# Log-sum-exp over heads: seven batches' results in one store behind the loads, and hand-named waits on the x buffers

## The chip, the cores and the metric

One core of one Trainium2 chip. The metric is the device time of one execution in microseconds (us), the median of 10 runs. All arithmetic is float32 except a bias that is split into bfloat16 parts.

## What is computed

```python
B, S, D, H = 8, 2048, 2048, 8
x_heads = x.reshape(B, S, H, D // H).transpose(0, 2, 1, 3)
x_heads = x_heads + bias[None, :, None, :]
x_tiled = np.repeat(x_heads, 2, axis=2)
mx = x_tiled.max(axis=-1, keepdims=True)
lse = mx.squeeze(-1) + np.log(np.exp(x_tiled - mx).sum(axis=-1))
```

For each of 8 batches, 2048 rows and 8 heads, 256 numbers plus their head's bias go through exp, are summed, and the log of the sum is written twice in a row. The input is 134 MB, the output (8, 8, 4096) float32 is 1 MB. The kernel leaves out the maximum, since exp of these inputs does not overflow.

## The kernel before, in words

**Tiles and loads.** The work is cut into T = 64 tiles of 256 rows by 2048 columns (2 MB), 8 tiles to a batch. Each partition holds K = 2 rows. Nine buffers `xt0` to `xt8` (`NBUF`, line 17) take the tiles in turn. `load(t)` (line 101) issues one DMA for each piece of a tile, always from SyncE's queue (SP). Up to tile 56 a tile is one piece; from tile 57 on it is two halves of 1 MB (one for each row of a partition); the last tile is cut into six pieces of 256 to 512 KB (`LAST_CUTS`, line 29). The load of tile t+9 is issued after the last instruction that uses tile t (line 328).

**Who does what to a tile.** There are three modes (lines 23 to 27). In all of them the first `pe` heads are done by TensorE and ScalarE: `add_bias` (line 158) puts the bias into PSUM with a small bfloat16 matmul, adds x to it with a matmul by the identity (line 177), and `sum_biased` (line 186) takes exp of each head with the sum as a by-product (line 189). The heads from `g0` up get their bias from GpSimd, in place (`g_add`, line 204, recorded at 207), then exp in place on ScalarE (`later`, line 214, exp at 212) and a sum on VectorE (line 228). The heads between are exp'd without bias and weighted by exp(bias):
- BULK, tiles 0 to 48: pe=2, g0=4. Heads 2 and 3 are multiplied by their weight in place on VectorE (line 222) before the sum over heads 2 to 7 (line 228).
- MIXED, tiles 49 to 60: pe=1, g0=5. Heads 1 to 4 are weighted and summed by `weigh` (line 235), one custom VectorE instruction for each row and head (line 240) which writes the weighted values to one of two scratch buffers `junk` and the sum to the results.
- PROMPT, tiles 61 to 63: pe=2, g0=8. GpSimd has no part; heads 2 to 7 go through `weigh`.

**Results.** The sums of batch b are gathered in `R[b]`. Two tiles after a batch's last tile, `finish(b)` (line 251) transposes them on TensorE (line 258), takes the log on ScalarE into one of two buffers `res0`, `res1`, 64 partitions by 2 KB (line 268), and stores 128 KB from SP's queue (line 269). `finish_last` (line 274) does the same for batch 7 into `res_last` with a store of its own (line 283).

**What sets the order.** The order of each engine's instructions is the order in which the program issues them (`manual_schedule`, line 107). A framework adds the waits: it tracks who wrote and who read each buffer, and gives an instruction a semaphore wait for every engine and DMA it depends on. Work of the engine itself can be waited for too: VectorE's `weigh` waits for the earlier `weigh` that wrote the same `junk`. DMAs on SP take 8 semaphores in turn ("lanes"), and a DMA waits for the DMA eight places before it on SP. An instruction holds one wait itself; for more, EVENT_SEMAPHORE instructions stand in front of it. The stores of batches 0 to 5 stand on SP between loads: behind the load of tile 17, 25, 33, 41, 49 and the second half of 57. The store of batch 6 already stands behind all loads.

Of the kernel before, what the change touches and what calls it, by code (L numbers as in the profile page):

```python
# [9 lines left out]
F32 = mybir.dt.float32  # L10
BF16 = mybir.dt.bfloat16
ACT = mybir.ActivationFunctionType
# [3 lines left out]
K = 2  # L16
NBUF = 9
# [15 lines left out]
def kernel(  # L33
# [6 lines left out]
    nc = tc.nc  # L40
    P = nc.NUM_PARTITIONS
    B, S, D = x.shape
    H, Dh = bias.shape
    assert D == H * Dh and S % (P * K) == 0
    NBLK = S // (P * K)
    T = B * NBLK
# [5 lines left out]
    sb = ctx.enter_context(tc.tile_pool(name="sb", bufs=1))  # L52
# [13 lines left out]

    R = [sb.tile([P, K, H, NBLK], F32, name=f"R{b}") for b in range(B - 1)]
    R_last = sb.tile([P, H, NBLK, K], F32, name="R_last")
    junk = [sb.tile([P, Dh], F32, name=f"junk{i}") for i in range(2)]
    res = [sb.tile([H * NBLK, P, K, 2], F32, name=f"res{i}") for i in range(2)]  # L70
    res_last = sb.tile([P, P, 2], F32, name="res_last")
    xts = [sb.tile([P, K, D], F32, name=f"xt{i}") for i in range(NBUF)]
    w_ps = pp.tile([P, W1 - W0], F32, name="w_ps")
# [4 lines left out]
    def mode_of(t):  # L78
        return [m for t0, m, _ in STAGES if t0 <= t][-1]

    def halves_of(t):
        return [s for t0, _, s in STAGES if t0 <= t][-1]

    def pieces(t):

        if not halves_of(t):
            return [(0, K, 0, D)]
        cuts = [[0, D]] * K if t < T - 1 else LAST_CUTS
        return [
            (k, k + 1, c0, c1) for k in range(K) for c0, c1 in zip(cuts[k], cuts[k][1:])  # L90
        ]

    def rows_of(t):

        b, blk = divmod(t, NBLK)
        v = x[b, blk * P * K : (blk + 1) * P * K, :]
        if b < B - 1:
            return v.rearrange("(p k) d -> p k d", k=K)
        return v.rearrange("(k p) d -> p k d", k=K)

    def load(t):
        for k0, k1, c0, c1 in pieces(t):
            nc.sync.dma_start(  # L103
                out=xts[t % NBUF][:, k0:k1, c0:c1], in_=rows_of(t)[:, k0:k1, c0:c1]
            )

    order = tc.manual_schedule()
# [3 lines left out]
    for set_idx, (_name, funcs) in enumerate(get_activation_tables(nc.m.arch).items()):  # L111
        if ACT.Exp in funcs and ACT.Ln in funcs:
            nc.scalar.add_instruction(
                mybir.InstLoadActFuncSet(
                    name=nc.get_next_instruction_name(),
# [5 lines left out]
    for t in range(NBUF):  # L121
        load(t)
# [20 lines left out]
    for i, c in enumerate(range(G0, D, MM)):  # L143
        spread(ps[i], c, c + MM)
        nc.scalar.activation(  # L145
            out=b_rep[:, c - G0 : c - G0 + MM], in_=ps[i], func=ACT.Copy
# [6 lines left out]


    n_ps = [0]
    n_junk = [0]

    def add_bias(m, xt, k0, k1):

        n = m["pe"] * Dh  # L160
        step = MM // n
        groups = [(k, min(k + step, k1)) for k in range(k0, k1, step)]
        got = []
        for ka, kb in groups:
            p = ps[n_ps[0] % len(ps)]
            n_ps[0] += 1
            nc.tensor.matmul(  # L167
                p[:, 0 : (kb - ka) * n],
                lhsT=ones3,
                rhs=each_row(b3, 0, n, kb - ka),  # L170
                start=True,
                stop=False,
            )
            got += [p[:, k * n : (k + 1) * n] for k in range(kb - ka)]
        for ka, kb in groups:
            p = got[ka - k0]
            nc.tensor.matmul(  # L177
                bass.AP(tensor=p.tensor, offset=p.offset, ap=[p.ap[0], [1, (kb - ka) * n]]),
                lhsT=ident,
                rhs=xt[:, ka:kb, 0:n],  # L180
                start=False,
                stop=True,
            )
        return got

    def sum_biased(m, p, dst):
        for h in range(m["pe"]):
            c = h * Dh
            nc.scalar.activation(  # L189
                out=p[:, c : c + Dh],  # L190
                in_=p[:, c : c + Dh],
                func=ACT.Exp,
                accum_out=dst(h),
            )

    def each_row(src, c, n, k_rows):

        return bass.AP(
            tensor=src.tensor,
            offset=src.offset + c,  # L200
            ap=[src.ap[0], [0, k_rows], [1, n]],
        )

    def g_add(m, xt, k0, k1):
        c = m["g0"] * Dh
        v = xt[:, k0:k1, c:D]
        nc.gpsimd.tensor_tensor(  # L207
            out=v, in0=v, in1=each_row(b_rep, c - G0, D - c, k1 - k0), op=ALU.add
        )

    def exp_inplace(v):
        nc.scalar.activation(out=v, in_=v, func=ACT.Exp)  # L212

    def later(m, xt, k0, k1, sums):

        h0 = m["pe"] if m["late"] else m["g0"]
        v = xt[:, k0:k1, h0 * Dh : D]
        exp_inplace(v)
        if m["late"]:
            n = (m["g0"] - h0) * Dh  # L220
            f = v[:, :, 0:n]
            nc.vector.tensor_tensor(  # L222
                out=f,
                in0=f,
                in1=each_row(w_ps, h0 * Dh - W0, n, k1 - k0),
                op=ALU.mult,
            )
        nc.vector.tensor_reduce(  # L228
            out=sums[:, k0:k1, h0:H],
            in_=v.rearrange("p k (h j) -> p k h j", j=Dh),  # L230
            op=ALU.add,
            axis=mybir.AxisListType.X,
        )

    def weigh(v, h, dst):
        c = h * Dh
        w = w_ps[:, c - W0 : c - W0 + Dh] if c < W1 else w_sb[:, c - W1 : c - W1 + Dh]
        j = junk[n_junk[0] % 2]
        n_junk[0] += 1
        nc.vector.tensor_tensor_reduce(  # L240
            out=j,
            in0=v,
            in1=w,
            scale=1.0,
            scalar=0.0,
            op0=ALU.mult,
            op1=ALU.add,
            accum_out=dst,
        )

    def finish(b):

        nr = H * NBLK
        n = P * K * 2
        tp = tps[b % 2]
        rs = res[b % 2]
        for k in range(K):
            nc.tensor.transpose(  # L258
                out=tp[0:nr, k],
                in_=R[b][:, k].rearrange("p h n -> p (h n)"),  # L260
                identity=ident,
            )
        tv = bass.AP(
            tensor=tp.tensor,
            offset=tp.offset,
            ap=[[tp.ap[0][0], nr], [1, P], [P, K], [0, 2]],
        )
        nc.scalar.activation(out=rs[0:nr], in_=tv, func=ACT.Ln)  # L268
        nc.sync.dma_start(
            out=out[b].rearrange("h (n r) -> (h n) r", r=n),  # L270
            in_=rs[0:nr].rearrange("q p k r -> q (p k r)"),
        )

    def finish_last():
# [14 lines left out]
    def sums_of(t):  # L289

        b, blk = divmod(t, NBLK)
        if b < B - 1:
            return R[b][:, :, :, blk]
        return R_last[:, :, blk, :].rearrange("p h k -> p k h")
# [3 lines left out]
    for t in range(T):  # L298
        m = mode_of(t)
        xt = xts[t % NBUF]  # L300
        sums = sums_of(t)
        for k0, k1, c0, c1 in pieces(t):
            if c0 == 0:
                got = add_bias(m, xt, k0, k1)
                if m["g0"] < H:
                    g_add(m, xt, k0, k1)
            if for_pool:
                for_pool()
                for_pool = None
            h0 = max(c0 // Dh, m["pe"])  # L310
            h1 = min(c1 // Dh, m["g0"])
            if h0 < h1 and not m["late"]:
                exp_inplace(xt[:, k0:k1, h0 * Dh : h1 * Dh])
            if for_pe and (c0 == 0 or c1 == D):
                for_pe()
                for_pe = None
            if not m["late"]:
                for k in range(k0, k1):
                    for h in range(h0, h1):
                        weigh(  # L320
                            xt[:, k, h * Dh : (h + 1) * Dh], h, sums[:, k, h : h + 1]
                        )

            def pool_part(t=t, m=m, xt=xt, k0=k0, k1=k1, sums=sums):
                if m["g0"] < H:
                    later(m, xt, k0, k1, sums)
                if k1 == K and t + NBUF < T:
                    load(t + NBUF)

            def pe_part(m=m, got=got, k0=k0, k1=k1, sums=sums):  # L330
                for k in range(k0, k1):
                    sum_biased(m, got[k - k0], lambda h: sums[:, k, h : h + 1])

            for_pool = pool_part
            if c0 == 0:
                if m["g0"] < H:
                    pe_part()
                else:
                    for_pe = pe_part

        fb, at = divmod(t - 2, NBLK)
        if fb >= 0 and at == NBLK - 1:
            finish(fb)
    for_pe and for_pe()
    finish_last()

# [31 lines left out]
```

The softmax here doesn't subtract the row's maximum and nothing guards it: scores larger than these inputs give would overflow.

## Time and profile before

| | |
|---|---|
| median of 10 runs | 332.18 us (331.91 to 332.39) |
| the profiled execution's own time | 332.26 us |
| its span, first to last instruction | 330.5 us |
| DMA queue of SP (q1): share of 16 engines' span | 96.9% |
| HBM read, written | 134.23 MB, 1.05 MB |
| instructions in the trace | 2287 |
| VectorE's EVENT_SEMAPHORE at line 240 | 24 |
| SP's EVENT_SEMAPHORE at line 103 | 107, 17 to 28 ns each |
| GpSimd's EVENT_SEMAPHORE at line 207 | 53, 17 to 43 ns each |
| ScalarE's EVENT_SEMAPHORE at line 212 | 65, 17 ns each |

Engines are PE (TensorE), PEld (its weight loads), DVE (VectorE), ACT (ScalarE), POOL (GpSimd) and SP. A "q" behind an engine's name (SPq) is its instruction queue. In a row of the timeline come start, duration, engine and line, what is written and read, and in brackets the idle time before it on its engine and what ended it. Here 1.8 us of the execution lie outside the span. In the rows of stages (windows) the fields are the stage, its length, each engine's busy time with its number of instructions, TensorE's granted clock, the mean busy share of the 16 DMA engines, and GB/s.

### The profile page before, as it was taken

To read this page: it belongs to the slowest core of one execution; us is meant where nothing else is said; L and a number is where in the kernel's file an instruction comes from. 1 tells how busy PE (TensorE), PEld (TensorE's weight loads), DVE (VectorE), ACT (ScalarE), POOL (GpSimd) and SP (SyncE) were. 2 spreads that over 40 slices of the span, in tenths; PEclk is the share of its full clock that TensorE was granted. 3 is DMA by queue.
4 is the path that set the end of the run, shared out by engine and by line. 5 is a ranking of instruction groups with operands and counts; after the bars stand their busy time and mean duration, and the time that the engine had idled before them with its cause. 6 is when DMAs were issued, how large, how long until landed. Compare 5 with 4: busy or idle time off the path is not lost. (4 is left out here: it accounts for less than half of the span.)

```text
span 330.5 us, 2287 instructions
## 1 busy us (share of the span) xinstructions
PE 230.5 (70%) x383; PEld 66.0 (20%) x383; DVE 288.2 (87%) x380; ACT 291.3 (88%) x567; POOL 270.7 (82%) x79
## 2 busy tenths in 40 slices
PE   5499667676767689666896766967946545665790
PEld 2122211121211122211221221321211110132220
DVE  0019999999999999999999999989889999999994
ACT  2269999999999989989989999998999998999894
POOL 6999989979989999899999999988998667786300
PEclk9999896598777855898558777595697555555577
DMA  7999999999999999999999999999999999999970
GB/s 295 433 424 436 428 425 430 426 426 428 419 437 427 428 428 426 429 429 428 427 428 428 424 432 424 430 430 425 432 424 427 432 424 420 417 421 424 415 277 18
DMA packets 11745, 135.43 MB, mean 410 GB/s; under 512 B 1425, under 2 KB 1553, under 8 KB 2769
## 3 DMA queue, kind: packets, MB, share of 16 engines
q1 hardware_dynamic: 11632, 135.27, 96.9%
q14 instruction: 12, 0.10, 0.1%
q8 instruction: 3, 0.05, 0.1%
q10 hardware_dynamic: 2, 0.01, 0.0%
q0 software_dynamic: 96, 0.00, 0.0%
HBM read 134.23 MB, written 1.05 MB: 409 GB/s over the span
## 5 line engine op out<-in xcount | busy, mean ns | idle before, releaser
L207 POOL TENSOR_TENSOR xt<-xt,b_rep 128x2048 f32<-128x2048 f32 (+2 forms) x65 | 264.3, 4068 | 35.6 <-DMA xt<-in_x_dram 28.8
L177 PE MATMUL ps<-xt,ident 128*128 128x512 f32 (+1 forms) x240 | 175.9, 865 | 71.5 <-DMA xt<-in_x_dram 71.0
L212 ACT ACTIVATE xt<-xt 128x3072 f32<-128x3072 f32 (+3 forms) x89 | 184.6, 2095 | 9.6 <-POOL xt L207 7.7
L228 DVE TENSOR_REDUCE R<-xt 128x12 f32<-128x3072 f32 (+1 forms) x56 | 176.6, 3154 | 5.8 <-DVE xt L222 1.0
L189 ACT ACTIVATE ps<-ps 128x256 f32<-128x256 f32 x232 | 85.7, 369 | 15.9 <-PE ps L177 11.3
L222 DVE TENSOR_TENSOR xt<-xt,w_ps 128x1024 f32<-128x1024 f32 x49 | 59.6, 1217 | 30.0 <-ACT xt L212 29.9
L177 PEld LDWEIGHTS ps<-xt,ident 128*128 128x128 f32 x240 | 54.2, 255 | 153.2 <-DMA xt<-in_x_dram 110.1
L167 PE MATMUL ps<-b,ones 3*128 3x512 bf16 (+1 forms) x120 | 49.1, 473 | 9.0 <-ACT ps L189 5.3
L189 ACT ACTIVATION_READ_ACCUMULATOR ps<-ps 128x1 f32 x232 | 44.2, 190 | 0.0
L240 DVE CUSTOM_DVE_ANT_0 junk<-xt,w_ps 128x256 f32<-128x256 f32 x114 | 40.6, 418 | 1.2 <-ACT xt L212 1.1
L167 PEld LDWEIGHTS <-ones 3*128 3x128 bf16 x120 | 7.9, 98 | 80.2 <-issue 80.2
L228 DVE TENSOR_REDUCE R_last<-xt 128x3 f32<-128x768 f32 (+1 forms) x9 | 9.4, 1042 | 0.0
L258 PE MATMUL tpair<-ident,R 128*64 128x128 f32 x14 | 3.7, 361 | 7.5 <-DVE R L228 6.0
L240 DVE CUSTOM_DVE_ANT_0 junk<-xt,w_sb 128x256 f32<-128x256 f32 x18 | 6.7, 422 | 0.0
L240 DVE DVE_READ_ACCUMULATOR2_ANT R_last<- 128x1 f32 x76 | 6.5, 85 | 0.0
L139 PE MATMUL ps<-brow,ones 1*128 1x512 f32 x4 | 3.7, 1085 | 3.5 <-DMA brow<-in_bias_dram 3.5
L145 ACT ACTIVATE b_rep<-ps 128x512 f32<-128x512 f32 x2 | 1.2, 597 | 4.6 <-PE ps L139 4.6
L240 DVE DVE_READ_ACCUMULATOR2_ANT R<- 128x1 f32 x56 | 4.7, 85 | 0.0
L139 PE MATMUL w_ps<-brow,ones 1*128 1x512 f32 x4 | 4.0, 1094 | 0.7 <-ACT w_ps L151 0.7
L258 PEld LDWEIGHTS tpair<-ident,R 128*64 128x64 f32 x14 | 1.5, 138 | 14.3 <-DVE R L228 11.0
L268 ACT ACTIVATE res<-tpair 64x512 f32<-64x512 f32 x7 | 4.1, 581 | 0.2
L151 ACT ACTIVATE w_ps<-w_ps 128x512 f32<-128x512 f32 x2 | 1.2, 582 | 3.3 <-PE w_ps L139 3.3
(21 smaller groups left out, 12.4 us busy)
## 6 DMA issues: line engine op xcount, KB each, us to landing
xt<-in_x_dram SPq DMA_DIRECT2D x57, 2048.0 KB, 31.7
xt<-in_x_dram SPq DMA_DIRECT2D x12, 1024.0 KB, 20.8
out_dram<-res SPq DMA_DIRECT2D x7, 128.0 KB, 31.0
xt<-in_x_dram SPq DMA_DIRECT2D x3, 256.0 KB, 15.7
xt<-in_x_dram SPq DMA_DIRECT2D x2, 384.0 KB, 15.9
xt<-in_x_dram SPq DMA_DIRECT2D x1, 512.0 KB, 12.3
out_dram<-res_last SPq DMA_DIRECT2D x1, 128.0 KB, 1.7
b<-bparts POOLq DMA_DIRECT2D x3, 1.0 KB, 5.6
```

The costliest lines, as they stand in the source:

```text
L139: nc.tensor.matmul(dst, lhsT=ones, rhs=brow[:, c0:c1], start=True, stop=True)
L145: nc.scalar.activation(out=b_rep[:, c - G0 : c - G0 + MM], in_=ps[i], func=ACT.Copy)
L167: nc.tensor.matmul(p[:, 0 : (kb - ka) * n], lhsT=ones3, rhs=each_row(b3, 0, n, kb - ka), start=True, stop=False,)
L177: nc.tensor.matmul(bass.AP(tensor=p.tensor, offset=p.offset, ap=[p.ap[0], [1, (kb - ka) * n]]), lhsT=ident, rhs=xt[:, ka:kb, 0:n], start=F ...
L189: nc.scalar.activation(out=p[:, c : c + Dh], in_=p[:, c : c + Dh], func=ACT.Exp, accum_out=dst(h),)
L207: nc.gpsimd.tensor_tensor(out=v, in0=v, in1=each_row(b_rep, c - G0, D - c, k1 - k0), op=ALU.add)
L212: nc.scalar.activation(out=v, in_=v, func=ACT.Exp)
L222: nc.vector.tensor_tensor(out=f, in0=f, in1=each_row(w_ps, h0 * Dh - W0, n, k1 - k0), op=ALU.mult,)
L228: nc.vector.tensor_reduce(out=sums[:, k0:k1, h0:H], in_=v.rearrange("p k (h j) -> p k h j", j=Dh), op=ALU.add, axis=mybir.AxisListType.X,)
L240: nc.vector.tensor_tensor_reduce(out=j, in0=v, in1=w, scale=1.0, scalar=0.0, op0=ALU.mult, op1=ALU.add, accum_out=dst,)
L258: nc.tensor.transpose(out=tp[0:nr, k], in_=R[b][:, k].rearrange("p h n -> p (h n)"), identity=ident,)
L268: nc.scalar.activation(out=rs[0:nr], in_=tv, func=ACT.Ln)
```

## The change

Three edits. First, `res` becomes one buffer of 64 partitions by 7 batches by 2 KB, `finish(b)` only writes its part of it, and one new `store()`, called after `finish(6)`, stores all seven batches in a single DMA of 896 KB (64 x 7 rows of 512 numbers). It stands on SP behind all loads and before the last batch's store. Second, `weigh` writes the weighted values in place instead of to `junk`. Third, every instruction that touches an x buffer goes through `on_x`, which keeps only the named waits: the load for the first toucher, the instruction before it for the next ones, and the last readers (`last_uses`) for the load that reuses the buffer. The instructions of PE, ACT, DVE and POOL and their order stay as they were; on SP the six stores between loads go.

```diff
-    junk = [sb.tile([P, Dh], F32, name=f"junk{i}") for i in range(2)]
-    res = [sb.tile([H * NBLK, P, K, 2], F32, name=f"res{i}") for i in range(2)]
+    res = sb.tile([H * NBLK, B - 1, P, K, 2], F32, name="res")
...
+    def on_x(t, ins, after):
+        known = [u for u in users[t] if u.ins.engine != ins.ins.engine]
+        for before in range(t % NBUF, t, NBUF):
+            known += users[before]
+        for u in known:
+            if u not in after:
+                tc.declare_no_dep(
+                    ins.ins, u.ins, reason="waited for by those it waits for"
+                )
+        users[t].append(ins)
+        return ins
...
     def load(t):
+        after = last_uses[t - NBUF] if t >= NBUF else []
         for k0, k1, c0, c1 in pieces(t):
-            nc.sync.dma_start(
-                out=xts[t % NBUF][:, k0:k1, c0:c1], in_=rows_of(t)[:, k0:k1, c0:c1]
+            loads[t, k0, c0] = on_x(
+                t,
+                nc.sync.dma_start(
+                    out=xts[t % NBUF][:, k0:k1, c0:c1],
+                    in_=rows_of(t)[:, k0:k1, c0:c1],
+                ),
+                after,
             )
...
-        nc.vector.tensor_tensor_reduce(
-            out=j,
+        ttr = nc.vector.tensor_tensor_reduce(
+            out=v,
...
+        last_uses[t].append(on_x(t, ttr, [after]))
...
-        nc.scalar.activation(out=rs[0:nr], in_=tv, func=ACT.Ln)
+        nc.scalar.activation(out=res[:, b], in_=tv, func=ACT.Ln)
+
+    def store():
+
         nc.sync.dma_start(
-            out=out[b].rearrange("h (n r) -> (h n) r", r=n),
-            in_=rs[0:nr].rearrange("q p k r -> q (p k r)"),
+            out=out[0 : B - 1].rearrange("b h (n r) -> (h n) b r", n=NBLK),
+            in_=res.rearrange("q b p k r -> q b (p k r)"),
         )
...
             finish(fb)
+            if fb == B - 2:
+                store()
```

The waits that this leaves, counted in the two built programs beyond the one that each instruction holds: SP 170 before, 115 after; DVE 141 and 0; POOL 102 and 1; ACT 70 and 2; PE 6 and 6.

More of the change, by code (lines that the diff above doesn't have):

```diff
@@ L99, in rows_of @@
         return v.rearrange("(k p) d -> p k d", k=K)
+    users = [[] for _ in range(T)]
+    def on_x(t, ins, after):
[9 more added lines that the diff above has]
+        return ins
+    loads = {}
+    last_uses = [[] for _ in range(T)]
     def load(t):
+        after = last_uses[t - NBUF] if t >= NBUF else []
         for k0, k1, c0, c1 in pieces(t):
-            nc.sync.dma_start(
-                out=xts[t % NBUF][:, k0:k1, c0:c1], in_=rows_of(t)[:, k0:k1, c0:c1]
+            loads[t, k0, c0] = on_x(
[5 more added lines that the diff above has]
+                after,
             )
@@ L155, with add_bias @@
     n_ps = [0]
-    n_junk = [0]
-    def add_bias(m, xt, k0, k1):
+    def add_bias(m, t, k0, k1):
         n = m["pe"] * Dh
+        xt = xts[t % NBUF]
         step = MM // n
@@ L176, in add_bias @@
             p = got[ka - k0]
-            nc.tensor.matmul(
-                bass.AP(tensor=p.tensor, offset=p.offset, ap=[p.ap[0], [1, (kb - ka) * n]]),
+            mm = nc.tensor.matmul(
+                bass.AP(
+                    tensor=p.tensor,
+                    offset=p.offset,
+                    ap=[p.ap[0], [1, (kb - ka) * n]],
+                ),
                 lhsT=ident,
@@ L183, in add_bias @@
             )
+            last_uses[t].append(on_x(t, mm, [loads[t, k0, 0]]))
         return got
@@ L202, in each_row, with g_add, exp_inplace, later @@
         )
-    def g_add(m, xt, k0, k1):
+    def g_add(m, t, k0, k1):
         c = m["g0"] * Dh
-        v = xt[:, k0:k1, c:D]
-        nc.gpsimd.tensor_tensor(
+        v = xts[t % NBUF][:, k0:k1, c:D]
+        add = nc.gpsimd.tensor_tensor(
             out=v, in0=v, in1=each_row(b_rep, c - G0, D - c, k1 - k0), op=ALU.add
         )
-    def exp_inplace(v):
-        nc.scalar.activation(out=v, in_=v, func=ACT.Exp)
-    def later(m, xt, k0, k1, sums):
+        return on_x(t, add, [loads[t, k0, 0]])
+    def exp_inplace(t, v, after):
+        return on_x(t, nc.scalar.activation(out=v, in_=v, func=ACT.Exp), [after])
+    def later(m, t, k0, k1, sums, add):
         h0 = m["pe"] if m["late"] else m["g0"]
-        v = xt[:, k0:k1, h0 * Dh : D]
-        exp_inplace(v)
+        v = xts[t % NBUF][:, k0:k1, h0 * Dh : D]
+        done = exp_inplace(t, v, add)
         if m["late"]:
@@ L221, in later @@
             f = v[:, :, 0:n]
-            nc.vector.tensor_tensor(
+            mul = nc.vector.tensor_tensor(
                 out=f,
@@ L227, in later @@
             )
-        nc.vector.tensor_reduce(
+            done = on_x(t, mul, [done])
+        red = nc.vector.tensor_reduce(
             out=sums[:, k0:k1, h0:H],
@@ L233, in later, with weigh @@
         )
-    def weigh(v, h, dst):
+        last_uses[t].append(on_x(t, red, [done]))
+    def weigh(t, v, h, dst, after):
         c = h * Dh
         w = w_ps[:, c - W0 : c - W0 + Dh] if c < W1 else w_sb[:, c - W1 : c - W1 + Dh]
-        j = junk[n_junk[0] % 2]
-        n_junk[0] += 1
-        nc.vector.tensor_tensor_reduce(
-            out=j,
+        ttr = nc.vector.tensor_tensor_reduce(
+            out=v,
             in0=v,
@@ L249, in weigh @@
         )
+        last_uses[t].append(on_x(t, ttr, [after]))
     def finish(b):
         nr = H * NBLK
-        n = P * K * 2
         tp = tps[b % 2]
-        rs = res[b % 2]
         for k in range(K):
@@ L302 @@
         for k0, k1, c0, c1 in pieces(t):
+            add = None
             if c0 == 0:
-                got = add_bias(m, xt, k0, k1)
+                got = add_bias(m, t, k0, k1)
                 if m["g0"] < H:
-                    g_add(m, xt, k0, k1)
+                    add = g_add(m, t, k0, k1)
             if for_pool:
@@ L312 @@
             if h0 < h1 and not m["late"]:
-                exp_inplace(xt[:, k0:k1, h0 * Dh : h1 * Dh])
+                done = exp_inplace(
+                    t, xt[:, k0:k1, h0 * Dh : h1 * Dh], loads[t, k0, c0]
+                )
             if for_pe and (c0 == 0 or c1 == D):
@@ L320, with pool_part @@
                         weigh(
-                            xt[:, k, h * Dh : (h + 1) * Dh], h, sums[:, k, h : h + 1]
-                        )
-            def pool_part(t=t, m=m, xt=xt, k0=k0, k1=k1, sums=sums):
-                if m["g0"] < H:
-                    later(m, xt, k0, k1, sums)
+                            t,
+                            xt[:, k, h * Dh : (h + 1) * Dh],
+                            h,
+                            sums[:, k, h : h + 1],
+                            done,
+                        )
+            def pool_part(t=t, m=m, k0=k0, k1=k1, sums=sums, add=add):
+                if add:
+                    later(m, t, k0, k1, sums, add)
                 if k1 == K and t + NBUF < T:
```

## The prediction

> **What bounds the kernel now.** I read the page first. Every engine but one is 70 to 88% busy, which settles nothing; the DMA row stands at nine tenths from the second slice to the 38th, and the GB/s row lies between 415 and 437 over the slices 2 to 38.
>
> ```profile
> PE 230.5 (70%) x383; PEld 66.0 (20%) x383; DVE 288.2 (87%) x380; ACT 291.3 (88%) x567; POOL 270.7 (82%) x79
> ...
> DMA  7999999999999999999999999999999999999970
> ...
> q14 instruction: 12, 0.10, 0.1%
> q8 instruction: 3, 0.05, 0.1%
> ...
> out_dram<-res SPq DMA_DIRECT2D x7, 128.0 KB, 31.0
> out_dram<-res_last SPq DMA_DIRECT2D x1, 128.0 KB, 1.7
> ```
>
> Then GpSimd's rows in the timeline. Its bias add needs nothing but the load, so its starts are the landings of the tiles:
>
> ```profile
> 88.57 4.55 POOL L207 TENSOR_TENSOR xt<-xt,b_rep 128x2048 f32<-128x2048 f32 x1 [0.38 <-DMA xt<-in_x_dram]
> 93.46 4.54 POOL L207 TENSOR_TENSOR xt<-xt,b_rep 128x2048 f32<-128x2048 f32 x1 [0.34 <-DMA xt<-in_x_dram]
> 98.67 4.55 POOL L207 TENSOR_TENSOR xt<-xt,b_rep 128x2048 f32<-128x2048 f32 x1 [0.67 <-DMA xt<-in_x_dram]
> ```
>
> The step is 4.89 us a tile, 2 MB at 429 GB/s, and it is 5.21 where a store has passed through the queue (store 0 was issued at 65.80, and a store lands 31.0 after its issue). The same 0.67 of idle stands at 138.12 and 177.68 and 0.64 at 217.12, behind stores 1, 2 and 3. The stream is never short of work: a 2 MB load lands 31.7 us after its issue, six tiles deep.
>
> Last the tail, by the stages of one us, and VectorE's rows with idle time in the timeline:
>
> ```profile
> 318.00:319.00 1.00, 1.00 (x2) 0.00 (x0) 0.72 (x5) 1.00 (x2) 0.00 (x0) 0.62 0.95 351
> 319.00:320.00 1.00, 1.00 (x3) 0.39 (x3) 1.00 (x7) 0.97 (x6) 0.00 (x0) 1.00 0.39 148
> 320.00:321.00 1.00, 1.00 (x4) 0.19 (x2) 0.98 (x6) 0.97 (x4) 0.00 (x0) 1.00 0.25 96
> 321.00:322.00 1.00, 1.00 (x2) 0.20 (x2) 0.65 (x3) 1.00 (x3) 0.00 (x0) 1.00 0.14 53
> 322.00:323.00 1.00, 0.03 (x1) 0.00 (x0) 1.00 (x7) 0.97 (x6) 0.00 (x0) 1.00 0.05 20
> ```
> ```profile
> 254.54 1.22 DVE L222 TENSOR_TENSOR xt<-xt,w_ps 128x1024 f32<-128x1024 f32 x1 [0.17 <-ACT xt L212]
> ...
> 318.83 0.42 DVE L240 CUSTOM_DVE_ANT_0 junk<-xt,w_ps 128x256 f32<-128x256 f32 x1 [0.28 <-ACT xt L212]
> ...
> 321.35 0.42 DVE L240 CUSTOM_DVE_ANT_0 junk<-xt,w_ps 128x256 f32<-128x256 f32 x1 [0.37 <-ACT xt L212]
> ...
> 323.92 0.42 DVE L240 CUSTOM_DVE_ANT_0 junk<-xt,w_ps 128x256 f32<-128x256 f32 x1 [0.42 <-ACT xt L212]
> ```
>
> Two things are to be seen. The DMA share doesn't drop at once at the end: it falls from 0.95 to 0.05 over four us, so a few of the 16 engines are up to four us behind the others, and a piece has landed only when its last engine is done. And VectorE has no listed idle time between 254.54 and 318.83; before that it waits for ScalarE, ScalarE for GpSimd and GpSimd for the load in almost every tile. The chain of waits says how it ends: the piece of the last tile that lands at 320.22 releases an exp on ScalarE, and from there ScalarE and VectorE work through to 326.1, transpose, log, and the store issued at 327.11.
>
> **The stores taken out of the stream.** Six of the seven stand between loads; the seventh already is behind them. The added step is 0.32 three times, and 0.29 at 217.12 (217.12 - 211.93 = 5.19 against 4.89); 128 KB at 429 GB/s is 0.31, so there is no more in it than bytes. Six by 0.32 = 1.9 us off the landing of the last pieces. All 16 engines carry an equal share (64 rows by 2 KB), so the late engines gain it too. Here a rule speaks for far more. The Trainium skill, "DMA: Bandwidth & Descriptors", section "Anatomy of one DMA — SWDGE (gpsimd) path", gives a DMA some 2.0 us fixed and bytes/436e3, measured on GpSimd's path. By it six stores would be 6 x 2.3 = 13.8 us. The row says 0.32 each, because the fixed part is a latency that the queued loads cover; I take the row.
>
> SP loses six issues (0.47 us each in the timeline) and the waits for the log ahead of them. SP runs six tiles ahead, so this is worth nothing by itself.
>
> **The big store.** It is 7 x 0.32 = 2.2 us of DMA time behind the last load. The last engine ends its loads at about 322.9 (share 0.05 in the last stage), in the new kernel some 2 us earlier, so the store is through at 320.9 + 2.2 = 323.1. The last batch's store, behind it on SP and in the rings, is issued at 327.1 - 2 = 325.1: two us of cover, cost nothing. A rule speaks against it: rows 2 KB wide now lie 128 KB apart, and the skill's page on DMA, "Latency and other measured facts", has copies with a large power of two as row pitch lose rate (207 GB/s at 512 KiB, 164 at 2 MiB, 103 at 4 MiB, with 214 as full rate). At half our rate the store takes 4.4 us and ends at 325.3, about even; at a quarter 8.8 us and ends at 329.7. But 128 KB is below the rule's first figure, which is nearly full rate, so I take 2.2, with 0 as the low bound of the cost (nothing can end before the last batch) and +4.6 as the high one. Its issue on SP makes 448 rows instead of 64: between 0.47 and, if it went by rows, 3.3 us; it is issued at about 313 and SP has nothing else to do until 325.
>
> **In-place `weigh`.** 132 instructions of 418 to 422 ns, one every 0.34 us with its read. The nearest row for a write to the place just read is the in-place multiply: 1217 ns for 1024 numbers, where the sum of 3072 takes 3355. The slope (3355 - 1217)/2048 = 1.044 ns predicts both with the same 148 ns start, so in place costs nothing. Bounds: if the dropped wait for the earlier scratch write had held each step by 20 ns, 132 x 20 ns = 2.6 us of VectorE time; or as much lost. Of that only what lies behind the last exp counts, six steps: +-0.1 us.
>
> **Waits dropped.** About 365 waits go, by pairs and singly, some 290 EVENT_SEMAPHORE instructions of 17 to 43 ns on queues that run ahead of their engines. In the bulk they are hidden by the load stream; if the cover were gone, GpSimd's 53 would be worth 53 x 43 ns = 2.3 us in all. On the last chain one counts, the 0.02 us at ScalarE's queue: 0. No new wait is added. But they have a second effect that I weigh more: the program shrinks by about 290 of 2287 instructions, and instructions are fetched through the same DMA engines. The trace's own DMA records have an instruction packet of 8 KB at 42.6, of 16 KB at 71.2 (1.10 us long) and of 8 KB at 225.1. GpSimd's idle time just behind them is 0.67 (48.07), 1.57 (73.86) and 1.03 (227.58) where 0.35 is usual, and the step that follows is not shorter: one engine stays behind. That is where the four us of the tail come from, 0.9 of them there from the first tile on by the landings of its 16 shares. By the instruction counts ScalarE's block number five (near 298, +0.66 us on the latest engine) and VectorE's number four (near 318, +0.25) fall past the end when ScalarE has 644 - 68 and VectorE 508 - 122 instructions. That would be another 0.9. Which engine a packet lands on may be dealt anew, though: bounds -1.5 to +0.8.
>
> **What is late next.** 1.9 + 0.9 = 2.8 off the loads can't all be had. VectorE's unbroken stretch starts at a tile (48) that four stores precede, so it starts 4 x 0.32 = 1.3 earlier; besides that it has only its idle 0.28 + 0.37 + 0.42 = 1.1 us to give. Cap: 2.4 us. ScalarE has 0.85 and 0.17 of waits for loads at 312 and 315 behind a tile with five stores ahead: 1.6 + 1.0 = 2.6, a little more. So the sum is 2.4 us: 332.26 - 2.4 = 329.9 (332.18, the median, is 0.08 below the profiled run; I leave it out).
>
> **Rivals.**
> - Stores alone: the fetches cost the latest engine what they cost now, or more by one packet. 332.26 - 1.9 = 330.4, with one more hit of 0.66 331.0. For it: nobody says where a packet goes. Against: two fetches less.
> - Fetches dealt better from the start, so that VectorE's stretch starts earlier too: 329.2. For it: the hits at 48, 74 and 227 were all on the latest engine, which is unlucky.
> - The gain is given back: VectorE, unbroken over 64 us, takes no benefit of stores 4 and 5, and its in-place steps cost a few ns each: 332.26 - 1.3 + 132 x 5 ns = 331.6 or up to 332.3. Against: the in-place multiply, and its 1.1 us of idle.
> - Slower: the big store holds up the last one. Place: the rings behind the last load; price: its time beyond 4.2 us (320.9 to 325.1), that is from a rate under about 215 GB/s. At a quarter of the rate 329.9 + 4.6 = 334.5. Against: stores in the stream went at the loads' rate.
>
> **How the numbers follow.** Both terms, capped: 0.57, 329.9. Stores alone: 0.25, 330.4 to 331.0. Better dealt: 0.08, 329.2. Given back: 0.05, 331.6 to 332.3. Slower: 0.05, 334.5. Range 329.1 to 331.0: it leaves out the last two and a bit of the tails. Within 0.2% (0.66 us, 331.5 to 332.8, about what can be told from no change here) lies the fourth, slower the fifth: faster 0.90, same 0.05, slower 0.05.
>
> **What would show it.** GpSimd's step 4.89 where now 5.2 stands behind each store; fewer instruction packets on q14 and a steeper fall of the DMA share at the end; VectorE's idle times in the last tile gone or nearly; the big store landing before the last one is issued. I am wrong if the late engines fall further behind (a tail of the DMA share over five us or more), if weigh's step leaves 0.34, or if the last store lands more than 2 us after its issue.

## The result and the profile after

The changed kernel takes 329.48 us (median of 8, 329.36 to 329.70) against 332.25 for the kernel before (median of 28): ratio 0.9917, 95% interval 0.9909 to 0.9926, 2.8 us faster. The forecast was 329.9 in a range of 329.1 to 331.0. The profiled execution took 329.5 with a span of 327.7, against 332.26 and 330.5.

From the page of the changed kernel: the DMA row, the instruction queues, and the two stores that are left.

```profile
DMA  7999999999999999999999999999999999999991
...
q8 instruction: 3, 0.05, 0.1%
q14 instruction: 9, 0.07, 0.1%
...
out_dram<-res SPq DMA_DIRECT2D x1, 896.0 KB, 9.7
out_dram<-res_last SPq DMA_DIRECT2D x1, 128.0 KB, 1.7
```

The stream is as dense as it was, and q14 has carried 9 packets instead of 12, the last of which came at 330.2, behind all loads. GpSimd's starts, from the timeline, are again the landings of the tiles:

```profile
92.94 4.54 POOL L237 TENSOR_TENSOR xt<-xt,b_rep 128x2048 f32<-128x2048 f32 x1 [0.35 <-DMA xt<-in_x_dram]
97.83 4.53 POOL L237 TENSOR_TENSOR xt<-xt,b_rep 128x2048 f32<-128x2048 f32 x1 [0.36 <-DMA xt<-in_x_dram]
102.73 4.54 POOL L237 TENSOR_TENSOR xt<-xt,b_rep 128x2048 f32<-128x2048 f32 x1 [0.37 <-DMA xt<-in_x_dram]
...
171.27 4.55 POOL L237 TENSOR_TENSOR xt<-xt,b_rep 128x2048 f32<-128x2048 f32 x1 [0.35 <-DMA xt<-in_x_dram]
176.79 4.53 POOL L237 TENSOR_TENSOR xt<-xt,b_rep 128x2048 f32<-128x2048 f32 x1 [0.98 <-DMA xt<-in_x_dram]
```

The step of 5.21 behind each store is gone: 4.89 and 4.90 go on. A step of 5.52 remains at 176.79; in the trace's DMA records two instruction packets, at 173.1 and 175.1, stand just ahead of it.

The tail by stages of one us, and VectorE's rows with idle time:

```profile
318.00:319.00 1.00, 1.00 (x2) 0.31 (x2) 1.00 (x7) 1.00 (x3) 0.00 (x0) 0.50 0.97 381
319.00:320.00 1.00, 1.00 (x4) 0.29 (x3) 0.99 (x7) 1.00 (x3) 0.00 (x0) 0.96 0.48 186
320.00:321.00 1.00, 0.92 (x2) 0.10 (x1) 1.00 (x7) 0.97 (x5) 0.00 (x0) 1.00 0.23 88
321.00:322.00 1.00, 0.00 (x0) 0.00 (x0) 0.58 (x3) 1.00 (x2) 0.00 (x0) 1.00 0.12 47
322.00:323.00 1.00, 0.00 (x0) 0.00 (x0) 1.00 (x7) 0.97 (x5) 0.00 (x0) 0.75 0.00 0
```
```profile
253.38 1.22 DVE L253 TENSOR_TENSOR xt<-xt,w_ps 128x1024 f32<-128x1024 f32 x1 [0.95 <-ACT xt L243]
...
321.76 0.42 DVE L271 CUSTOM_DVE_ANT_0 xt<-xt,w_ps 128x256 f32<-128x256 f32 x1 [0.42 <-ACT xt L243]
```

The DMA share still tails off over three to four us, but now the big store is in that tail: it lands at 312.63 + 9.7 = 322.4, while the last piece of x has landed at 320.2. VectorE starts its unbroken stretch 1.2 us earlier and has one wait left instead of three. The chain of waits (start, duration, what) shows who sets the end:

```profile
295.19 19.95 DMA xt<-in_x_dram
315.16 1.49 ACT xt L243
316.64 0.40 ACT ps L219 x2
317.06 0.87 ACT ps L219 x4
317.96 0.47 ACT ps L219 x2
318.43 1.46 ACT xt L243 x2
319.89 0.40 ACT ps L219 x2
320.31 0.47 ACT ps L219 x2
320.79 0.95 ACT xt L243
321.76 0.42 DVE xt L271
```

The last load that ScalarE stands waiting for is the second half of tile 62, at 315.14; from there it works without a pause for 6.6 us, then VectorE does its six last steps. In the kernel before the same half landed at 317.29, and ScalarE's exp of it follows at once:

```profile
317.31 1.48 ACT L212 ACTIVATE xt<-xt 128x1536 f32<-128x1536 f32 x1
```

The last store was issued at 327.11 there; now it is at 324.96. So 2.15 us were gained up to the last store's issue, all of it by that landing: from this landing to the issue it is 9.82 us in both kernels. It is 9.82 to 9.84 in eight of the ten experiments below too; the others are the stores issued twice (9.99) and the reordered sums (9.31). The other 0.6 lie behind the issue: from there to the end of the span it is 330.46 - 327.11 = 3.35 before and 327.70 - 324.96 = 2.74 after.

Each load lands in 16 shares, one for each DMA engine. Three values worked out from their landings in the trace serve below: when the middle share landed (the mean of the eighth and the ninth), when the last one did, and their difference, the lateness of the last engine. For the last piece of x they are 319.38, 322.76 and 3.38 before, 317.51, 320.19 and 2.68 after. For the half of tile 62 the middle share came 1.87 earlier too, and the lateness fell from 3.13 to 2.84; the two make up the 2.15.

### The profile page after: what moved, and what is told of

It reads as the page before. It is cut to its first block, busy times and chain, and to the rows that moved or that the text cites. A ratio compares the mean times of both kernels' runs of the same rounds, so it can differ in the third digit from the quotient of the medians.

```text
span 327.7 us, 1984 instructions
## 1 busy us (share of the span) xinstructions
PE 236.8 (72%) x383; PEld 68.6 (21%) x383; DVE 288.7 (88%) x380; ACT 290.9 (89%) x567; POOL 270.7 (83%) x79
## 4 chain that ended last, share of the span: by engine, by line
DMA 66%; DVE 17%; ACT 7%; POOL 4%; PE 4%; issue 1%; SPq 0%; DVEq 0%
DMA xt<-in_x_dram 63%; DVE R L260 12%; ACT xt L243 5%; DVE xt L253 4%; PE ps L202 3%; POOL xt L237 3%; DMA b<-bparts 2%; ACT ps L219 2%; DVE xt L271 1%; DMA brow<-in_bias_dram 0%; POOL brest L157 0%; POOL brest L155 0%; POOL b L160 0%; PE ps L192 0%; POOL bparts L154 0%
## 5 line engine op out<-in xcount | busy, mean ns | idle before, releaser
L202 PE MATMUL ps<-xt,ident 128*128 128x512 f32 (+1 forms) x240 | 182.5, 895 | 73.0 <-DMA xt<-in_x_dram 72.3
L202 PEld LDWEIGHTS ps<-xt,ident 128*128 128x128 f32 x240 | 56.3, 265 | 153.2 <-DMA xt<-in_x_dram 111.9
L271 DVE CUSTOM_DVE_ANT_0 xt<-xt,w_ps 128x256 f32<-128x256 f32 x114 | 40.7, 422 | 0.4 <-ACT xt L243 0.4
L271 DVE CUSTOM_DVE_ANT_0 xt<-xt,w_sb 128x256 f32<-128x256 f32 x18 | 6.7, 430 | 0.0
```

Source lines behind the costliest of these rows:

```text
L202: mm = nc.tensor.matmul(bass.AP(tensor=p.tensor, offset=p.offset, ap=[p.ap[0], [1, (kb - ka) * n]],), lhsT=ident, rhs=xt[:, ka:kb, 0:n], s ...
L271: ttr = nc.vector.tensor_tensor_reduce(out=v, in0=v, in1=w, scale=1.0, scalar=0.0, op0=ALU.mult, op1=ALU.add, accum_out=dst,)
```

## The experiments

The theory: the end is set by the landings; stores among the loads cost their bytes; fewer instructions mean fewer instruction packets, and the last engine is less late. The rivals: the waits themselves were what cost; a DMA has a fixed cost that merging saves; the in-place writes or the place of the big store matter.

**One part at a time.** The store part alone, on the kernel before:

```diff
-    res = [sb.tile([H * NBLK, P, K, 2], F32, name=f"res{i}") for i in range(2)]
+    res = sb.tile([H * NBLK, B - 1, P, K, 2], F32, name="res")
...
             finish(fb)
+            if fb == B - 2:
+                store()
```

> The store part alone: seven batches' results stay in SBUF and leave in one store behind the loads; the waits and the scratch buffers of weigh are those of before. By the theory that the loads' landing sets the end and each store between loads costs it its bytes, 6 x 0.32 = 1.9 us go: ratio 0.994 (330.3 us). By the rival that the dropped waits did it, ratio 1.000. By the rival that a DMA costs some 2 us fixed, 0.96.

Measured: 329.82 us, ratio 0.9934 (0.992 to 0.9947), 2.2 us. In its profile the middle share of the last piece landed at 317.80, 1.6 earlier than before, with a lateness of 3.47, as before. The last store was issued 1.6 earlier (325.52), and the end behind it is shorter by 0.6. So the stores are worth what was expected of them, 1.6 to 1.9, and the rest is at the end.

The waits and the in-place writes alone: the changed kernel with the seven stores of before (the parts with the two buffers are left out).

```diff
-        nc.scalar.activation(out=res[:, b], in_=tv, func=ACT.Ln)
-
-    def store():
-
+        nc.scalar.activation(out=rs[0:nr], in_=tv, func=ACT.Ln)
         nc.sync.dma_start(
-            out=out[0 : B - 1].rearrange("b h (n r) -> (h n) b r", n=NBLK),
-            in_=res.rearrange("q b p k r -> q b (p k r)"),
+            out=out[b].rearrange("h (n r) -> (h n) r", r=n),
+            in_=rs[0:nr].rearrange("q p k r -> q (p k r)"),
         )
...
             finish(fb)
-            if fb == B - 2:
-                store()
```

> The other part alone: the hand-named waits and weigh in place, with the seven stores of before. By the theory it takes about 290 instructions out, so fewer instruction packets run on the DMA engines and the latest engine is less late: 0.3 to 0.9 us, ratio 0.997 to 0.999. By the rival that waits cost their own queue time on the path, about 2.7 us, ratio 0.992. By a theory that only bytes count, 1.000.

Measured: 331.29 us, ratio 0.9975 (0.9966 to 0.9984), 0.8 us. The middle share of the last piece landed at 319.39, within 0.01 us of before: the waits themselves bought the stream nothing. The lateness fell from 3.38 to 2.29. In its profile, which at 331.06 us lies 0.2 under the median, the second half of tile 62 landed 0.71 earlier than before, at 316.58, and the end behind the last store's issue is shorter by 0.47 (2.88 against 3.35). So a good part of the 0.8 lies at the end and is no gain of the loads. The instruction queues:

```profile
q8 instruction: 3, 0.05, 0.1%
q14 instruction: 10, 0.08, 0.1%
```

The two parts add up to 3.0, a little more than the 2.8 of both together: each shortens the end, by 0.6 and 0.47, and together they shorten it by 0.6 once.

**Place or merging.** The changed kernel with seven stores in a row at the end:

```diff
-    def store():
+    def store(b):

         nc.sync.dma_start(
-            out=out[0 : B - 1].rearrange("b h (n r) -> (h n) b r", n=NBLK),
-            in_=res.rearrange("q b p k r -> q b (p k r)"),
+            out=out[b].rearrange("h (n r) -> (h n) r", n=NBLK),
+            in_=res[:, b].rearrange("q p k r -> q (p k r)"),
         )
...
             if fb == B - 2:
-                store()
+                for i in range(B - 1):
+                    store(i)
```

> The changed kernel with seven stores of 128 KB in a row behind the loads instead of one of 896 KB. By the theory that it is the place that counts, the time of the changed kernel, ratio to before 0.991 to 0.992. By the rival that merging counts (a fixed cost for each DMA), later by 6 x 0.5 to 2 us: 1.000 or above. Seven stores also take seven of the eight turns on SP's semaphores, so the last store waits for a load eight places back either way.

Measured: 329.48 us, ratio 0.9922 (0.991 to 0.9935): the changed kernel's time. The seven stores land 0.25 to 0.38 us apart, 2.2 us in all, as the big one does (322.38 - 320.19 = 2.19). Merging shows no gain; the gain of the store part is that of its place. (The half of tile 62 landed 0.17 earlier here than in the changed kernel, and the end is 0.13 longer for a reason given below, so a gain of merging of some 0.1 us could hide.)

**More stores among the loads.** Twice on the kernel before. First each store issued twice:

```diff
+        for _ in range(2 if b < B - 2 else 1):
+            nc.sync.dma_start(
...
```

> The kernel before, with each store of batches 0 to 5 issued twice in a row (same bytes to the same place). By the theory 6 x 0.32 = 1.9 us are added, less what ScalarE's and VectorE's lag hides: ratio 1.005 to 1.006. By the rival that the stores lie hidden between loads, 1.000. By a fixed cost of 2 us each, 1.04.

Measured: 354.35 us, ratio 1.0674 (1.0659 to 1.0688), 22 us more, far off each expectation. The waits of SP's own queue name the reason:

```profile
SPq L270 <- DMA out_dram<-res: 178.0, 6, 34.6
```

The framework makes the second store wait for the first, since both write the same place. Six times SP stood for up to 34.6 us with the next loads queued behind it. That is not the cost of a store, so the run says nothing on it, but a lot on what a wait on SP in front of the loads would have cost. It also tells where the lateness comes from. At the fourth of these waits the queue ran nearly empty (the DMA share is 0.07 from 222 to 224 us), and the lateness fell from 2.22 at the load before it to 0.44 at the load behind it; at the last piece it is 1.02, not 3.38. An engine that had fallen behind caught up when the queue ran out of work. In the next run the second copy goes to the place of the next batch's results:

```diff
+        if b < B - 2:
+            nc.sync.dma_start(
+                out=out[b + 1].rearrange("h (n r) -> (h n) r", r=n),
+                in_=rs[0:nr].rearrange("q p k r -> q (p k r)"),
+            )
```

> The kernel before with a second store of the same 128 KB behind each store of batches 0 to 5, to the place of the next batch's results, which that batch's own store overwrites some 39 us later, so that no store waits for the one just ahead. By the theory that a store costs its bytes in the queue, 6 x 0.3 = 1.8 us more, ratio 1.0055. If two small DMAs in a row slow the loads beside them, as in the run with the small loads, 4 to 7 us more, 1.012 to 1.022.

Measured: 333.93 us, ratio 1.0055 (1.0042 to 1.0069), 1.8 us, as expected. GpSimd's rows around the first pair of stores:

```profile
93.08 4.54 POOL L207 TENSOR_TENSOR xt<-xt,b_rep 128x2048 f32<-128x2048 f32 x1 [0.36 <-ACT ps L189]
98.58 4.54 POOL L207 TENSOR_TENSOR xt<-xt,b_rep 128x2048 f32<-128x2048 f32 x1 [0.97 <-DMA xt<-in_x_dram]
```

The idle time is 0.97 where one store gave 0.67 and none 0.36: 0.30 for each store.

**More bytes, as loads.** The same with a small load instead of a store:

```diff
+    more = [sb.tile([H * NBLK, 512], F32, name=f"more{i}") for i in range(2)]
...
+        if b < B - 2:
+            nc.sync.dma_start(out=more[b % 2], in_=x[b, 0:nr, 0:512])
```

> The kernel before with one more load of 128 KB (64 rows of 2 KB into a scratch buffer) behind each of the stores of batches 0 to 5, in place of the doubled stores, which waited for each other. By the theory that bytes in the queue set the end, 6 x 0.31 = 1.9 us more, ratio 1.0055. By a fixed cost of 2 us a DMA, 1.04; hidden, 1.000.

Measured: 339.63 us, ratio 1.0221 (1.0207 to 1.0235), 7.4 us: a miss of the byte theory for small loads. At the last piece the middle share came 5.8 later than before, and the lateness grew from 3.4 to 5.1, so the small loads held up all engines, and the last one more. Since the rows read lay 8 KB apart, the next run read one unbroken stretch:

```diff
+        if b < B - 2:
+            nc.sync.dma_start(
+                out=more[b % 2],
+                in_=x[b, 0 : nr // 4, :].rearrange("s (c d) -> (s c) d", d=512),
+            )
```

> The kernel before with one more load of 128 KB behind each of the stores of batches 0 to 5, read from one unbroken stretch of memory, where the run with the small loads read rows of 2 KB, 8 KB apart. If the broken rows made those loads dear, 1.8 us more, ratio 1.0055. If any small load among the large ones is, 7 us more, ratio 1.022.

Measured: 338.87 us, ratio 1.0204 (1.0189 to 1.0219). So it isn't the broken rows. GpSimd's rows around the first store and load:

```profile
88.27 4.53 POOL L208 TENSOR_TENSOR xt<-xt,b_rep 128x2048 f32<-128x2048 f32 x1 [0.34 <-ACT ps L190]
93.72 4.54 POOL L208 TENSOR_TENSOR xt<-xt,b_rep 128x2048 f32<-128x2048 f32 x1 [0.92 <-DMA xt<-in_x_dram]
99.36 4.53 POOL L208 TENSOR_TENSOR xt<-xt,b_rep 128x2048 f32<-128x2048 f32 x1 [1.10 <-DMA xt<-in_x_dram]
```

The steps on both sides of the pair are 5.45 and 5.64, together 1.3 over 2 x 4.89, where a store alone adds 0.3. In the DMA records of the first of the two runs the 16 KB packets around the small load take up to 0.96 us (near 91.8) and 1.11 (near 131.6) instead of 0.61. Why a small load slows the large ones and a small store doesn't is open; in both runs the small loads filled 64 partitions, and no run varies that.

**In place or not.** The changed kernel with the scratch buffers and their wait:

```diff
+        j = junk[n_junk[0] % 2]
+        n_junk[0] += 1
         ttr = nc.vector.tensor_tensor_reduce(
-            out=v,
+            out=j,
...
```

> The changed kernel, but weigh writes to the two scratch buffers as before and so keeps its wait for the scratch write two steps back. If writing in place costs or saves nothing, as the prediction has it, the step of weigh stays 0.34 us and the ratio to before is the changed kernel's, 0.9915 to 0.992. By the rival that the in-place write slows VectorE by some ns a step, a step nearer to 0.33 and 0.1 us less at the end; by the one that the wait cost something, 0.35.

Measured: 329.37 us, ratio 0.9914 (0.9901 to 0.9928): no difference, and the step of `weigh` is 0.34 us in both. The instruction takes 415 ns there, and 422 in the changed kernel, but 411 in the run with seven late stores, which also writes in place: that spread is no effect of the target.

**More instructions.** The changed kernel with memsets on GpSimd:

```diff
+    pad = sb.tile([P, 12], F32, name="pad")
...
+        for i in range(6 if m["late"] else 12):
+            nc.gpsimd.memset(pad[:, i : i + 1], 0.0)
```

> The changed kernel with 6 tiny memsets on GpSimd behind the bias add of each tile up to 48 and 12 behind each of the 16 later ones, some 490 instructions that nobody waits for[...]. GpSimd has 0.35 us idle a tile. By the theory that instruction packets make one DMA engine late, about four more packets stand on q14, each with a jump of 0.3 to 0.7 us of one engine behind it, and the end moves later by 0 to 1.3 us according to which engine they meet. By the rival that only waits and stores count, nothing moves unless GpSimd's starts leave the landings.

Measured: 329.62 us, ratio 0.9926 (0.9912 to 0.9939), 0.1 over the changed kernel, within the interval. From its page:

```profile
q14 instruction: 12, 0.10, 0.1%
q8 instruction: 3, 0.05, 0.1%
```

Three more packets came with the instructions. But the lateness at the last piece is 2.32, not more than the 2.68 of the changed kernel, and the last store was issued 0.24 earlier (324.72). So the number of packets alone doesn't set the lateness. By the theory a packet counts when it meets the engine that is last already: the packets at 209.7 and 278.9, where the changed kernel has none, raised the lateness by 0.2 for one load only. What this run loses, it loses at the end, which is 3.07 us long and not 2.74: a gap of 0.37 stands behind GpSimd's 580th recorded instruction, where the changed kernel has 0.06 between the same two.

**A version that beats both.** The profile after says that ScalarE sets the last 6.6 us. In the last tile I put its sums of TensorE's heads behind all exps:

```diff
-            if for_pe and (c0 == 0 or c1 == D):
-                for_pe()
+            if for_pe and (c0 == 0 or c1 == D) and not (t == T - 1 and k0 == 0 and c0):
+                if t == T - 1 and k0 == 1 and c0 == 0:
+                    held = for_pe
+                else:
+                    for_pe()
                 for_pe = None
...
+    held()
     for_pe and for_pe()
```

> The changed kernel, but in the last tile ScalarE does the sums of TensorE's two heads of both rows behind all of its exps instead of between them. By the theory that the last 6.6 us are ScalarE's work without a pause, VectorE's last wait of 0.42 us goes, and the end comes 0.3 to 0.4 us earlier: ratio to before 0.9905. By the rival that the last load still sets the end, nothing.

Measured: 329.01 us, ratio 0.9902 (0.9889 to 0.9916), 0.5 under the changed kernel's 329.48 (its slowest run took 329.06, the fastest of the changed kernel 329.36), and the last store is issued at 324.49 instead of 324.96. ScalarE's row and VectorE's one with idle time, in the timeline:

```profile
318.38 3.03 ACT L243 ACTIVATE xt<-xt 128x768 f32<-128x768 f32 x4
```
```profile
319.24 0.42 DVE L271 CUSTOM_DVE_ANT_0 xt<-xt,w_ps 128x256 f32<-128x256 f32 x1 [0.18 <-ACT xt L243]
```

Four exps in a row, and VectorE's last wait of 0.42 is gone; 0.18 is left. The landing of the last piece doesn't set the end.

## Why the prediction was right, point by point

**Stores out of the stream, 1.9.** Right. The middle share of the last piece came 1.87 earlier, with 0.03 of it at the first tile; in the five other kernels without stores among the loads it came 1.6 to 1.8 earlier, and six more stores made it 1.8 later. Merging showed no gain, and each store among the loads cost 0.3 us: the fixed 2.0 us that the prediction weighed do not show in a queue that is always full.

**Waits dropped, 0; fewer instruction packets, 0.9.** The waits themselves: right, they moved the middle share by 0.01. The packets: the direction was right, the size too large. The two packets named, ScalarE's near 298 and VectorE's near 318, stand in the kernel before, where the lateness rises by 0.68 and 0.25 at them. But the half of tile 62, which sets the end, lands before VectorE's packet comes, so that one could not count. At this half the lateness fell by 3.13 - 2.84 = 0.3 in the changed kernel. In the other kernels with the dropped waits it is 2.37 to 2.78, and in two that kept them (the store part alone, the second stores) 3.12 and 2.97: a gain of 0.1 to 0.8, with one profile of each. Which packet meets the last engine is luck: in the run with the second stores ScalarE's packet (at 300.2) raised the lateness by nothing and VectorE's (at 319.1) by 1.0, and the padded program has three more packets and no more lateness.

**The chain and the cap, VectorE at 2.4.** The prediction let the end start with the piece that lands at 320.22. ScalarE had been at work without a pause since 317.31 and came to the next exps only at 320.49, so this landing held up nothing; the one at 317.29 did. The cap was about the right size and on the wrong engine. I gave ScalarE 2.6 by counting its waits of 0.85 and 0.17 for loads as room. They are no room: they are waits for the loads of tiles 61 and 62, and such waits are still there after (0.86 and 0.18, at 310.12 and 315.16). ScalarE's stretch without a pause begins at the second half of tile 62, and that moved by 2.15. VectorE kept 0.42 of its idle time, which the reordered sums then took.

**What I had not in the sum: the end, 0.6.** The mechanism of the prediction gave 2.15 of the measured 2.8, where it had summed 2.4; the other 0.6 came where I expected nothing, and that is luck. In the kernel before, the closing instructions on SP hold a gap of 0.36 us behind SP's 207th recorded instruction, and the kernel has 211 of them. The same gap stands behind the 207th in the runs with added loads and added stores (0.35 to 0.37), which also have more than 207; the kernels with fewer (199, 162, 150) end without it. A like gap of 0.42 to 0.45 stands behind SP's 79th recorded instruction, 128 earlier, in eleven of the twelve traces, at 125.4 us in the kernel before and at 184.2 in the changed one; in the twelfth a longer wait covers the place. So the gap goes by the count of instructions and not by what they do, which fits a step from one instruction block to the next; that was not tried by itself. With what stands around it the gap is worth 0.47: by that much the run with the waits alone, whose order of waits is the old one, shortens the end. The other 0.13 is the row of waits that SP ends with, one every 0.07 us over the semaphores of its DMAs in a fixed order: the last store's turn moved two places towards the end of that row. The run with the waits alone and the one with seven late stores have the old turn, and 2.88 and 2.87 us behind the issue instead of 2.74.

**The big store.** It took 2.19 us against 2.2 forecast, and it landed 2.6 us before the last store was issued. Rows 128 KB apart cost it no rate. Its issue took 0.71 us on an SP with nothing behind it.

**In-place `weigh`.** Nothing, as forecast. The prediction's own ground was weak: it took the slope and the start of 148 ns from two rows, and then said that they fit these two rows, as two points always do. The run that kept the scratch buffers is the test.

**The signs.** GpSimd's step, the packets on q14, the early landing of the big store and the unchanged step of `weigh` came as named, and the last store landed 1.7 us after its issue. The steeper fall of the DMA share is not to be seen, since the big store fills that stretch.

**The rivals.** Stores alone: the run is 329.8, 0.6 below the 330.4 that I gave it, by the end that I didn't know. Fetches dealt better, with VectorE's stretch earlier too: the stretch began 1.16 earlier, no more than the four stores ahead of it explain. Given back, and slower: not seen. The stores issued twice show what the slower side would have looked like had the store stood with its wait ahead of loads.

## What to carry to other kernels

In a kernel that its load stream bounds, as this one, a store between loads costs its bytes, and moved behind the last load it is free if it is through before the last store is issued; merging it added nothing. Waits that are implied by others cost the stream nothing here, but each is an instruction that is fetched through the same DMA engines, and the last of 16 engines sets every landing. What that is worth depends on which engine a packet meets, so it can't be forecast to better than some tenths of a us. When counting how far a tail can move, a wait for a load is no room for that load: look which landing starts the last stretch without a pause, and on which engine.

## What the runs showed of the hardware

- An instruction packet of 8 KB can hold up a DMA engine by more than its own 0.31 us: in the kernel before, the 16 KB data packet that began at 93.31, as the instruction packet of 93.0 ended, took 1.27 us instead of 0.61. The lateness of the last engine is 0.38 us at the first tile there and rises at the packets of 42.6 (to 0.71), 71.1 (16 KB, to 1.94), 225.1 (to 2.57), 297.8 (to 3.12) and 318.2 (to 3.42); between them it changes by 0.13 at most from load to load. The other nine packets before the last piece did not raise it. It fell back to 0.4 where the queue ran nearly empty (the stores issued twice).
- A load of 128 KB (64 partitions by 2 KB) among loads of 2 MB cost 1.1 to 1.2 us (6.8/6 and 7.4/6), a store of the same size and shape 0.3. Why is open.
- In a full queue a store of 128 KB lands 0.30 to 0.36 us behind the load ahead of it, and a second store 0.30 to 0.32 behind the first: no fixed cost is seen. The last store, with the queue empty, lands 1.7 us after its issue.
- SP shows a gap of some 0.4 us behind its 79th and its 207th recorded instruction, 128 apart, whatever they are.
